# A float32 transformer-like block on one core: the low parts of one weight matrix made by an accumulating DMA instead of a VectorE subtraction

## The chip, the cores and the metric

The kernel runs on one core of a Trainium2 chip. The metric is the device time of one execution in microseconds (us). TensorE (PE) multiplies matrices, VectorE (DVE) and ScalarE (ACT) work element by element, GpSimd (POOL) does small work and can issue DMAs, SyncE (SP) issues nearly all of the DMAs. PEq, ACTq, SPq and POOLq in the profile are the engines' instruction queues.

## The reference, cut to what matters

Two layers (DEPTH = 2) work on 256 tokens of width 1024. Each layer has a feed-forward part, a mixer, a cross attention and a second feed-forward part, each followed by a layer norm. The change lies in the mixer's input product:

```
z = h @ w_in[l]                                   # 256 x 1024 by 1024 x 3072
cb, cc, ch, rq, rf, ri, rg, pu = jnp.split(z, split_at, axis=-1)
y_rec = hgrn2(rq, rf, ri, rg, lbs[l], rec_norm_g[l])   # the recurrence; rq are its queries
```

The 512 columns of w_in that give rq begin at column 768. They are the query weights of the title.

## The kernel before, in words

**Two parts for each float32 factor.** PE multiplies in the format fp32r, which keeps fewer bits than float32. So each factor is split in a rounded part and a rest: `split` (line 60) lets ACT copy the source into the rounded part (line 61, `whi` for weights) and DVE subtract the rounded part from the source (line 62, `wlo`). A product is the sum of three: high by high, high by low, low by high. `product` (line 103) issues all of these matmuls, so that they all stand at line 106.

**Loading weights.** `load` (line 64) brings in a block of 1024 rows by 512 columns as two DMAs of 1 MB on SP (line 76) into `raw`, a ring of 3 buffers. Each raw buffer is split in two halves of 128 x 1024 elements. So a block of 512 columns has four halves, and each half is one ACT copy, one DVE subtraction, one `whi` buffer and one `wlo` buffer, from two rings of 8. Half number n (0 to 3) holds the rows k = 2n and 2n + 1 of the eight groups of 128 rows.

**Products by columns.** In the mixer (line 592) `columns` (line 596) loads a block and then calls `mm_cols` (line 115) for each group of 128 columns. `mm_cols` runs in this order: seven matmuls of `whi` with both parts of the input (k = 0 to 6, 128x512), eight of `wlo` with the input's high part (k = 0 to 7, 128x256), and the last of `whi`. `add` (line 124) then takes the sum out of PSUM: an ACT copy (line 126) and a DVE addition (line 127). The PSUM tiles named `acc` are a ring of 4 buffers.

**Order of the work around the change.** In each layer PE does, one after the other: the end of the first feed-forward part, the keys' first block (`keys`, with `mT`), the four column groups of f (line 628, columns 1280 to 1791; ACT applies a sigmoid at line 617 and DVE makes f and k at lines 619 and 623), the four column groups of q (line 630, columns 768 to 1279, the recurrence's queries), and then the values and the other columns, woven with the recurrence's small matmuls (lines 701 and 736). A scheduler decides the order of each engine's instructions; each engine then runs its own in that order and waits at semaphores. The loads run ahead of the products: while PE multiplies f, the weights of q are split, and the raw weights of the values (columns 1792 on) and of the pool (columns 2816 on) are fetched.

**What POOL does.** It issues 38 small DMAs in the first 50 us, and later runs the power for each layer norm (line 327) and for the recurrence (line 801).

Of the kernel before, what the change touches and what calls it, by code (L numbers as in the profile page):

```python
# [12 lines left out]
ALU = mybir.AluOpType  # L13
# [4 lines left out]
P = 128  # L18
# [5 lines left out]
NK = DM // P  # L24
# [22 lines left out]
def model(ctx: ExitStack, tc: tile.TileContext, t: dict, out: bass.AP):  # L47
    nc = tc.nc
# [11 lines left out]
    def split(hi, lo, src):  # L60
        nc.scalar.copy(hi, src)  # L61
        lows.append(nc.vector.tensor_tensor(lo, src, hi.bitcast(F32), op=ALU.subtract))  # L62

    def load(src, k0, nk, c0, ncol, fine=False, strewn=False):

        hi, lo, todo = [], [], []
        step = 2048 // ncol
        for a in range(k0, k0 + nk, step):  # L70
            raw = wp.tile([P, 2048], F32, tag="raw", name="raw", bufs=3)
            raw = raw.rearrange("p (k c) -> p k c", c=ncol)
            half = step // 2
            part = 1 if fine else step
            for b in range(0, step, part):
                loads.append(nc.sync.dma_start(
                    raw[:, b : b + part, :],
                    src[:, c0 : c0 + ncol].rearrange("(p k) c -> p k c", p=P)[:, a + b : a + b + part, :]
                    if strewn
                    else src[(a + b) * P : (a + b + part) * P, c0 : c0 + ncol].rearrange("(k p) c -> p k c", p=P),  # L80
                ))
            for s in range(2):
                h = wp.tile([P, 1024], F32R, tag="whi", name="whi", bufs=8)
                w = wp.tile([P, 1024], F32R, tag="wlo", name="wlo", bufs=8)
                h = h.rearrange("p (k c) -> p k c", c=ncol)
                w = w.rearrange("p (k c) -> p k c", c=ncol)
                r = raw[:, s * half : (s + 1) * half, :]
                if fine:
                    todo += [(h[:, b, :], w[:, b, :], r[:, b, :]) for b in range(half)]
                else:  # L90
                    split(h, w, r)
                hi.append(h)
                lo.append(w)
        return Weights(hi, lo, half, todo)
# [20 lines left out]
    def mm_cols(w, cols, x):  # L115
        o = acc()
        for k in range(NK - 1):
            product(o, w.at(k, cols)[0], x[:, k], k == 0, False)
        for k in range(NK):
            product(o[:, 0, :], w.at(k, cols)[1], x[:, k, 0, :], False, False)  # L120
        product(o, w.at(NK - 1, cols)[0], x[:, NK - 1], False, True)
        return sums(o)
# [22 lines left out]
    h = [cst.tile([P, DM], F32, name=f"h{i}") for i in range(NT)]  # L145
# [230 lines left out]
    def ffn(l, name, n, pend=None, last=False, early=None):  # L376
        gate, up, down = (t[f"{name}_{x}"][l] for x in ("gate", "up", "down"))
        with tc.tile_pool(name="ffn", bufs=2, reuse_waits="tile") as fp:
# [45 lines left out]
            def first():  # L424

                s = activations()
                wg = load(gate, 0, NK, 0, CHUNK, fine=pend is None)
                wu = load(up, 0, NK, 0, CHUNK) if pend is not None else None

                if pend is None:  # L430
# [8 lines left out]
                    with tc.manual_schedule(engines={E.Activation, E.DVE, E.PE}):  # L439
# [21 lines left out]
                        for k in range(2, NK):  # L461
                            if k + 1 < NK:
                                split(*wg.todo[k + 1])
                            group(k, 0, 1)
                    wu = load(up, 0, NK, 0, CHUNK)
                    ou = all_products(wu)
                    for i in range(NT):
# [124 lines left out]
    def mixer(l, fill):  # L592
        w_in = t["w_in"][l]
        with tc.tile_pool(name="mix", bufs=1, reuse_waits="tile") as mp:

            def columns(c0, ncol, take, behind=lambda p: None, after=None):
                with tc.issue_after(after) if after is not None else nullcontext():
                    w = load(w_in, 0, NK, c0, ncol)
                for j in range(ncol // P):
                    take(j, mm_cols(w, slice(j * P, (j + 1) * P), xT))  # L600
                    if j % 2:
                        behind(j // 2)
                    yield
# [3 lines left out]
            k = mp.tile([P, NT, HEADS, P], F32, name="k")  # L607
# [20 lines left out]
            for _ in columns(1280, 512, lambda j, o: add(f[:, :, j, :], o), ev_f, normed[-1].ins):  # L628
                pass
            for _ in columns(768, 512, lambda j, o: add(q[:, :, j, :], o)):  # L630
                pass
# [36 lines left out]
            def between():  # L668
                yield from values_by_halves()
                yield from columns(2816, 256, lambda j, o: add_forward(pu[:, j, PAD:], o))  # L670
                yield from columns(0, 512, lambda j, o: add_forward(cv[j // 2][:, j % 2, :], o))
                yield from columns(512, 256, lambda j, o: add_forward(u[:, j, 2:], o))
# [51 lines left out]
            for n, c in enumerate(LEVELS):  # L724
                a = 64 // c
# [107 lines left out]
            src = pu  # L833
            for g, w_ in enumerate(WINDOWS):
# [9 lines left out]
                src = d  # L844
# [189 lines left out]
```

## Time and profile before

| what | us |
|---|---|
| median of 3 runs (lowest, highest) | 1090.08 (1089.45, 1090.17) |
| the profiled execution's own time | 1089.82 |
| its span, from first to last instruction | 1088.1 |
| PE busy | 1078.6 |
| DVE busy | 832.7 |
| ACT busy | 573.0 |
| POOL busy | 60.9 |

The span is the time from the first to the last instruction that the profiler recorded; about 1.7 us of the execution lie around it. A row of the timeline has the start in us, the busy time in us, the engine, the line, the operation, output and input tiles and shape, "xN" for N instructions merged into the row, and, in brackets, how long the engine was idle before the row and what ended that. A row of the windows has, for one stretch of the span, its length and then for each engine the busy time in it (with the number of instructions), the granted clock of PE as a share of the full clock, the mean busy share of the 16 DMA engines, and the rate in GB/s. Grouped rows have the number of instructions, the busy time in us and the mean ns of one.

### The profile page before, as it was taken

Reading aid. Unit: us, or ns where it says so; the run is one execution under the profiler, and the core shown is the slowest. Engines: PE = TensorE matmul, PEld = TensorE weight load, DVE = VectorE, ACT = ScalarE, POOL = GpSimd, SP = SyncE. Lnnn points to the kernel's source line nnn. Section 1 sums busy time; section 2 is a strip of 40 time slices with the busy share of each in tenths; the row PEclk is TensorE's granted clock in tenths of the full one; section 3 lists DMA queues with packets and bytes.
Section 4 is the critical chain, followed back from the end, with each engine's and each line's share of the span. In section 5 each row is a group of like instructions: output and inputs, shape, how many; then the busy total and the mean of one; then the engine's idle time right before and its main releaser. Section 6 shows DMA issues by size and latency. Waiting matters only on the chain.

```text
span 1088.1 us, 15589 instructions
## 1 busy us (share of the span) xinstructions
PE 1078.6 (99%) x6051; PEld 954.3 (88%) x6051; DVE 832.7 (77%) x1099; ACT 573.0 (53%) x795; POOL 60.9 (6%) x113
## 2 busy tenths in 40 slices
PE   9999999999999999999999999999999999999997
PEld 7888888989899888888888888898898998888886
DVE  6679677998988877666687655798989888765665
ACT  6456454766557454444455544456764654545450
POOL 9500001000000000000000000010000000000000
PEclk9999999999999999999999999999999999999999
DMA  9986664744475487766488666646536664966641
GB/s 329 300 285 224 220 213 157 247 178 175 173 274 175 164 279 225 236 215 213 155 267 265 222 200 220 227 164 234 185 122 225 235 222 155 286 218 213 221 164 39
DMA packets 122667, 231.85 MB, mean 213 GB/s; under 512 B 6305, under 2 KB 45505, under 8 KB 117473
## 3 DMA queue, kind: packets, MB, share of 16 engines
q1 hardware_dynamic: 120800, 228.48, 63.3%
q0 software_dynamic: 1216, 1.20, 0.4%
q8 instruction: 47, 0.77, 0.3%
q10 hardware_dynamic: 576, 1.18, 0.3%
q14 instruction: 28, 0.22, 0.1%
HBM read 216.15 MB, written 1.05 MB: 200 GB/s over the span
## 4 chain that ended last, share of the span: by engine, by line
PE 99%; DMA 0%; DVE 0%; issue 0%; DVEq 0%
PE acc L106 66%; PE dn L106 30%; PE acc L170 1%; PE dn L736 1%; DMA h<-in_x_dram 0%; PE dn L795 0%; PE dn L794 0%; PE dn L784 0%; PE acc L860 0%; PE dn L701 0%; PE dn L437 0%; DVE h L334 0%; DVE h L330 0%; DVE st L322 0%; DVE h L314 0%
## 5 line engine op out<-in xcount | busy, mean ns | idle before, releaser
L62 DVE TENSOR_TENSOR wlo<-raw,whi 128x1024 fp32r<-128x1024 f32 (+1 forms) x396 | 473.6, 1211 | 179.7 <-ACT whi L61 169.6
L61 ACT CAST whi<-raw 128x1024 fp32r<-128x1024 f32 (+1 forms) x396 | 402.5, 1041 | 334.8 <-PE dn L106 139.5
L106 PE MATMUL acc<-whi,xT 128*128 128x512 f32 x1312 | 395.0, 380 | 0.0
L106 PEld LDWEIGHTS acc<-whi,xT 128*128 128x128 f32 x1312 | 247.8, 189 | 35.2
L106 PE MATMUL acc<-wlo,xT 128*128 128x512 f32 x656 | 248.6, 379 | 0.0
L106 PE MATMUL acc<-xT,whi 128*128 128x512 f32 x576 | 142.1, 382 | 0.0
L106 PEld LDWEIGHTS acc<-wlo,xT 128*128 128x128 f32 x656 | 124.0, 189 | 17.4
L106 PE MATMUL dn<-whi,ah 128*128 128x512 f32 x346 | 131.5, 380 | 0.0
L106 PE MATMUL dn<-wlo,ah 128*128 128x512 f32 x346 | 131.1, 379 | 0.0
L106 PE MATMUL dn<-whi,al 128*128 128x512 f32 x346 | 131.1, 379 | 0.0
L106 PEld LDWEIGHTS acc<-xT,whi 128*128 128x128 f32 x576 | 104.1, 190 | 11.8
L106 PE MATMUL dn<-whi,xT 128*128 128x512 f32 x288 | 88.6, 382 | 0.0
L106 PEld LDWEIGHTS acc<-xT,wlo 128*128 128x128 f32 x576 | 75.5, 191 | 3.9
L106 PE MATMUL acc<-xT,wlo 128*128 128x256 f32 x576 | 75.9, 275 | 0.0
L106 PEld LDWEIGHTS dn<-whi,al 128*128 128x128 f32 x346 | 65.4, 189 | 9.3
L106 PEld LDWEIGHTS dn<-wlo,ah 128*128 128x128 f32 x346 | 65.4, 189 | 9.2
L106 PEld LDWEIGHTS dn<-whi,ah 128*128 128x128 f32 x346 | 65.4, 189 | 9.1
L418 DVE STREAM_TRANSPOSE square<-dealt 128x512 f32<-128x512 f32 x40 | 63.6, 1662 | 0.6 <-DMA dealt<-sg 0.5
L327 POOL TENSOR_TENSOR rs<-rs,nhalf 128x1 f32<-128x1 f32 x16 | 14.9, 929 | 853.7 <-DVE rs L326 853.7
L106 PEld LDWEIGHTS dn<-whi,xT 128*128 128x128 f32 x288 | 54.5, 190 | 7.7 <-DVE xT L62 0.3
L106 PE MATMUL dn<-wlo,xT 128*128 128x512 f32 x144 | 54.6, 379 | 0.0
L320 DVE SCALAR_TENSOR_TENSOR h<-h,dn 128x512 f32<-128x512 f32 x31 | 21.2, 683 | 29.8 <-PE dn L106 29.8
(205 smaller groups left out, 964.5 us busy)
## 6 DMA issues: line engine op xcount, KB each, us to landing
raw<-in_ffn_up_dram SPq DMA_DIRECT2D x44, 1024.0 KB, 5.0
raw<-in_ffn_down_dram SPq DMA_DIRECT2D x44, 1024.0 KB, 5.0
raw<-in_ffn_gate_dram SPq DMA_DIRECT2D x42, 1024.0 KB, 5.0
raw<-in_w_in_dram SPq DMA_DIRECT2D x24, 1024.0 KB, 5.0
dealt<-sg SPq DMA_DIRECT2D x80, 128.0 KB, 3.2
raw<-in_ca_k_dram SPq DMA_DIRECT2D x8, 1024.0 KB, 4.8
raw<-in_w_out_dram SPq DMA_DIRECT2D x8, 1024.0 KB, 4.8
raw<-in_ca_v_dram SPq DMA_DIRECT2D x8, 1024.0 KB, 4.9
```

Source lines behind the costliest of these rows:

```text
L61: nc.scalar.copy(hi, src)
L62: lows.append(nc.vector.tensor_tensor(lo, src, hi.bitcast(F32), op=ALU.subtract))
L106: nc.tensor.matmul(o, w, x, start=start, stop=stop)
L170: nc.tensor.transpose(pt[:, k, :], src[:, (4 * j + k) * P : (4 * j + k + 1) * P], unit)
L320: nc.vector.scalar_tensor_tensor(v, v, ALPHA / scale, sums(y[i][n]), op0=ALU.mult, op1=ALU.add)
L327: nc.gpsimd.tensor_tensor(rs, rs, nhalf[:, 0:1], op=ALU.pow)
L418: nc.vector.transpose(d.rearrange("p k (i b) -> p b k i", b=4), x[:, :, i, :].rearrange("p b (j k) -> p b k j", k=4))
L736: nc.tensor.matmul(o[g, hh, :], kc[:, hh, g], x, start=True, stop=True)
```

## The change

In each layer, for the block of w_in that begins at column 768 and for no other, the low part is no longer made by DVE. ACT writes the rounded part as before, then writes the source times -1, rounded, into the `wlo` buffer, and a DMA issued by POOL reads the same 512 KB of weights once more from HBM and adds them to what stands in `wlo`. The sum is the source less its rounded part, as before.

```diff
-    def load(src, k0, nk, c0, ncol, fine=False, strewn=False):
+    def load(src, k0, nk, c0, ncol, fine=False, strewn=False, summed=False):
...
-                if fine:
+                if summed:
+                    nc.scalar.copy(h, r)
+                    nc.scalar.mul(w, r, -1.0)
+                    nc.gpsimd.dma_start(
+                        w,
+                        src[(a + s * half) * P : (a + (s + 1) * half) * P, c0 : c0 + ncol].rearrange("(k p) c -> p k c", p=P),
+                        accum_op=ALU.add,
+                    )
+                elif fine:
...
-                    w = load(w_in, 0, NK, c0, ncol)
+                    w = load(w_in, 0, NK, c0, ncol, summed=c0 == 768)
```

A block has four halves and there are two layers, so the change concerns 8 halves in all. Built, the changed program has 8 DVE subtractions fewer, 8 ACT instructions more and 8 POOL DMAs more. PE's instructions and their order are the same; the first matmuls on `wlo` in the first column group of q wait for the DMAs where they waited for DVE. On POOL the four DMAs of a layer stand between the power of that layer's first norm (line 327) and the powers of its recurrence (line 801).

## The prediction

> **What bounds the kernel now.** I read the page first, then the windows, then the timelines around the queries' products. The page's busy times, and its chain of work that ended last:
>
> ```profile
> PE 1078.6 (99%) x6051; PEld 954.3 (88%) x6051; DVE 832.7 (77%) x1099; ACT 573.0 (53%) x795; POOL 60.9 (6%) x113
> ...
> PE 99%; DMA 0%; DVE 0%; issue 0%; DVEq 0%
> ```
>
> PE is the bound. The windows show where its idle 9.5 us lie:
>
> ```profile
> 0.00:10.00 10.00, 7.91 (x31) 6.25 (x32) 3.35 (x6) 4.41 (x7) 9.16 (x26) 1.00 0.81 296
> ...
> 192.00:213.00 21.00, 21.00 (x131) 19.29 (x130) 18.55 (x32) 15.13 (x23) 0.00 (x0) 1.00 0.83 278
> 213.00:265.00 52.00, 52.00 (x569) 45.77 (x568) 45.56 (x90) 34.96 (x72) 2.03 (x2) 1.00 0.48 171
> ...
> 950.00:1088.00 138.00, 130.66 (x639) 115.17 (x637) 89.64 (x99) 55.08 (x63) 1.84 (x2) 0.98 0.53 174
> ```
>
> 2.1 us are in the first ten, 7.3 us at the end; in between PE is full. So relief of DVE has next to nothing to win, and a wait that the change puts on PE is paid in full, since no later gap takes it up. The question is only whether the new low parts are there when PE reads them.
>
> **When PE reads them.** PE's timeline, layer 1, then layer 2 (a column group starts with seven `whi` matmuls):
>
> ```profile
> 202.49 1.89 PE L106 MATMUL acc<-xT,whi 128*128 128x512 f32 x8
> 204.22 1.05 PE L106 MATMUL acc<-xT,wlo 128*128 128x256 f32 x8
> 205.11 1.25 PE L106 MATMUL acc<-xT,whi 128*128 128x512 f32 x5
> ```
>
> ```profile
> 740.89 1.05 PE L106 MATMUL acc<-xT,wlo 128*128 128x256 f32 x8
> ```
>
> Eight `wlo` matmuls take 205.11 - 204.22 = 0.89 us, two to a half. Half 0 is read at 204.22, half 2 at 204.67, half 3 at 204.89; in layer 2 half 3 at 741.56.
>
> **Removed and added on DVE and ACT.** The groups between 189 and 206 us, by form:
>
> ```profile
> L62 DVE TENSOR_TENSOR wlo<-raw,whi 128x1024 fp32r<-128x1024 f32 x10 | 11.9, 1219 | 0.4 <-ACT whi L61 0.4
> ...
> L61 ACT CAST whi<-raw 128x1024 fp32r<-128x1024 f32 x8 | 8.0, 1052 | 0.8 <-DMA raw<-in_w_in_dram 0.7
> ...
> L617 ACT ACTIVATE f<-f 128x512 f32<-128x512 f32 x2 | 1.3, 636 | 0.3 <-DVE f L127 0.3
> ...
> L61 ACT CAST kTh<-sums 128x512 fp32r<-128x512 f32 x1 | 0.6, 618 | 0.0
> ```
>
> DVE loses 4 x 1.22 = 4.9 us a layer. On the path that is worth nothing, as PE is full. ACT gains four multiplications. The trace has none of 1024 elements; at 512 an ACTIVATE (636 ns) costs what a cast does (618), so I take the cast's 1.05 us, 4.2 us a layer. ACT is busy 15.13 of 21 us there, so it fits, but it moves the casts and copies behind it. ACT's timeline, and the order of the built program (cast, cast, multiply, copy of sums, multiply, cast of kTh, cast, copy of f, multiply, cast, multiply), give the issue times:
>
> ```profile
> 190.96 2.02 ACT L61 CAST whi<-raw 128x1024 fp32r<-128x1024 f32 x2
> 192.85 0.39 ACT L126 COPY sums<-acc 128x256 f32<-128x256 f32 x1
> 193.96 1.99 ACT L61 CAST whi<-raw 128x1024 fp32r<-128x1024 f32 x2 [0.71 <-DMA raw<-in_w_in_dram]
> ...
> 196.38 0.36 ACT L126 COPY f<-acc 128x256 f32<-128x256 f32 x1
> ```
>
> ```profile
> 729.53 0.40 ACT L126 COPY sums<-acc 128x256 f32<-128x256 f32 x1
> 732.00 1.99 ACT L61 CAST whi<-raw 128x1024 fp32r<-128x1024 f32 x2 [2.07 <-DMA raw<-in_w_in_dram]
> ```
>
> Back to back, each adds about 0.95 us (193.96 + 1.99: two in 1.99). From 192.85 the multiplications end at 193.9, 195.15, 197.85 and 199.75; in layer 2, from 729.53, at 730.6, 731.8, 734.45 and 736.35. The last leaves 5.14 and 5.21 us until PE wants half 3. The copies of f come up to about 3 us later. That costs nothing: the first column's copy ends near 197 while q's first group takes over that `acc` tile at 202.49, and each later group follows 2.6 us on. Were it not so, PE would wait for ACT, at most these 3 us.
>
> **POOL and SP.** POOL's 0 instructions in 192 to 213 (row above) mean that nothing of its own delays the issues; behind them come only the powers of the recurrence, after 213. SP's loads of `raw` that reuse the queries' buffers wait for ACT's multiplication instead of DVE's subtraction: 195.2 and 199.8 instead of the 196.11 and 199.3 below. That shift alone costs nothing, since SP's queue reaches these loads anyway and PE needs the values only at 213. But they are what the new DMAs meet:
>
> ```profile
> 189.11 0.38 SPq L76 DMA_DIRECT2D raw<-in_w_in_dram  x1
> ...
> 193.50 0.38 SPq L76 DMA_DIRECT2D raw<-in_w_in_dram  x1
> ...
> 196.11 3.57 SPq L76 DMA_DIRECT2D raw<-in_w_in_dram  x2
> ```
>
> **The price of an accumulating DMA.** The trace has none. Nearest rows, from the DMA issues, from the queues, and from POOL's loads of `m`:
>
> ```profile
> raw<-in_w_in_dram SPq DMA_DIRECT2D x24, 1024.0 KB, 5.0
> ...
> lng<-in_ln_g_dram SPq DMA_DIRECT2D x8, 512.0 KB, 4.0
> ...
> m<-in_mem_dram POOLq DMA_DIRECT2D x32, 32.0 KB, 6.7
> ```
>
> ```profile
> L186 POOL DMA_DIRECT2D m<-in_mem_dram x32: 582/582/634, 22.2 to 47.4; - x32
> ...
> DMA to landing us min/median/max: 3.6/6.7/8.3
> ```
>
> ```profile
> q1 hardware_dynamic: 120800, 228.48, 63.3%
> q0 software_dynamic: 1216, 1.20, 0.4%
> ```
>
> ```profile
> 189.00:190.00 1.00, 1.00 (x10) 0.97 (x8) 1.00 (x3) 0.27 (x1) 0.00 (x0) 1.00 0.07 29
> 190.00:191.00 1.00, 1.00 (x6) 0.87 (x6) 1.00 (x2) 1.00 (x4) 0.00 (x0) 1.00 0.74 133
> 199.00:200.00 1.00, 1.00 (x10) 1.00 (x9) 0.58 (x2) 0.73 (x2) 0.00 (x0) 1.00 1.07 416
> ```
>
> At a full share the engines move 416 GB/s: 1 MB (1.05e6 bytes) takes 2.5 us, 512 KB 1.26 us. A 1 MB load lands in 5.0: about 1.1 until it moves (the one that SP issues at 189.11), 2.5 moving, 1.4 at the end. POOL's smallest landing, 3.6 us for 32 KB, puts its fixed part near 3.5, so 2.1 before the data and 1.4 behind.
>
> *Low bound:* it moves like a plain copy, 1.26 us each, ahead of all other traffic. The last lands at 199.75 + 3.5 + 1.26 = 204.5, before 204.89: nothing. *Upper bound:* an addition needs both operands, so the DMA must read 512 KB from HBM and 512 KB of `wlo` too, as much as a 1 MB load: 2.5 us each, 10.1 for four. They cannot start before 193.9 + 2.1 = 196.0, and the values' two loads and the pool's (6 us left) share the engines half and half: 196.0 + 16.1 + 1.4 = 213.5, 8.6 us late. *Taken:* the double read, being that of the nearest row of its size in bytes read, and a fifth of the engines for SP's loads meanwhile. The share I chose between none and half: q0's packets held 1.20 MB / 1216 = about 1 KB of 128-byte rows, eight rows to one, while q1's held 1.9 KB, one row. If the queues take turns by packets, POOL's get more than half. Then 196.0 + 10.1 / 0.8 + 1.4 = 210.0, **5.1 us late**.
>
> The Trainium skill, "Collectives: The Full Stack", section "The bandwidth ceiling: the fold count and why AG ≠ RS ≠ AR", says that an add in the DMA path halves the rate because it reads two sources, not because the adding is slow. By it the upper price holds; without it the wait could be nothing. No run here shows it yet.
>
> Layer 2 has the same slack within 0.1 us, and PE and the DMA engines are as full:
>
> ```profile
> 729.00:742.00 13.00, 13.00 (x81) 11.93 (x80) 11.71 (x17) 10.20 (x16) 0.00 (x0) 1.00 0.82 289
> ```
>
> So I take the same wait. **Sum:** 2 x 5.1 = 10.2 on the profiled execution's 1089.8 gives 1100.0; the median of the runs lies 0.3 above that execution, so 1100.3.
>
> **The rivals.**
>
> *A, cheap transfers (27%).* For: the last issue leaves 5.1 us, and a plain 512 KB load lands in 4.0. Against: the engines are 83% busy there already, and POOL's DMAs landed late (6.7) where they were. With plain moves and half the engines, half 3 lands at 207.5: 0 to 2.6 us a layer, 1090.1 to 1095.3. More than half of this (15%) is up to 1.1 us a layer, within 0.2% in all (about the least that a measurement of this kernel tells from no change).
>
> *B, longer waits (18%).* For: the upper bound, 8.6 us a layer, or 1107.3. The new DMAs also hold up the values' raw loads, and ACT's casts of these stand ahead of the copies of q. And PE's clock falls when it idles:
>
> ```profile
> 1080.38 0.28 PE L106 MATMUL acc<-whi,al 128*128 128x256 f32 x1
> ```
>
> ```profile
> 1082.00:1084.00 2.00, 0.00 (x0) 0.00 (x0) 2.00 (x5) 0.00 (x0) 0.92 (x1) 0.79 0.00 0
> 1084.00:1088.00 4.00, 0.00 (x0) 0.00 (x0) 0.84 (x3) 0.00 (x0) 0.00 (x0) 0.50 0.37 133
> ```
>
> PE's last matmul ends at 1080.66; 0.79 means 1.0 until 1083.2, then 0.5: it fell after 2.5 us. In the forecast half 2 comes about 2.2 us late and half 3 keeps PE a further 2.9, so the clock is near its edge. Half speed for as long as it took to fall costs 1.25 a layer. With both, 2 x 9.9 = 19.7: 1109.8. Were the moves twice as slow again, 196.0 + 20.2 / 0.8 + 1.4 = 222.7, 17.8 late: 1125.7.
>
> The Trainium skill, "TensorE: Matmul & The Clock Gate", section "Part 1: The HAM clock gate (the 'warmup' mystery)", halves the clock after an idle window of about 3.4 us and restores it after as much work. By it a drop would cost an estimated 1.7 us a layer; the 2.5 us above fits only if such a window runs free of the matmuls.
>
> *C, faster (3%).* Mechanism: DVE, 4.9 us a layer ahead, ends waits of the recurrence's small matmuls, whose weight loads waited:
>
> ```profile
> PEld dn L736 <- issue: 2.5, 10, 0.3
> ...
> PEld dn L736 <- ACT whi L61: 0.7, 2, 0.3
> PEld dn L736 <- ACT win L843: 0.5, 2, 0.2
> ```
>
> If all 3.7 us went, 1086.4. It decides only if the transfers are wholly hidden, and against it stands that these loads run beside matmuls (PE 52.00 of 52.00).
>
> That the change does not do what it says is not open: the built order has no subtraction for these halves, and PE waits for the DMAs.
>
> **How the numbers follow.** Forecast 52%: 1095 to 1107, likeliest 1100.3. A 27%: 15 within 0.2%, 12 slower. B 18%. C 3%. So faster 0.03, same 0.15, slower 0.82. The range runs from 1090.1, where A begins, to 1112, just past B's 1109.8; C, some of A's hidden end, and B's slower transfers lie outside, less than 2 in 10.
>
> **What would show it.** PE idle ahead of the first `wlo` matmuls of q, near 204.5 and 741, twice 3 to 9 us, ended by DMAs into `wlo`; none there means A. POOL's new issues near 193.9, 195.2, 197.9 and 199.8; if they come later, ACT's walk is wrong. Landings of some 7 to 10 us under the raw loads; 4 to 5 means plain moves. DVE's busy total falls by 9.8 us, ACT's grows by 8.4. A granted clock below 1.00 behind the gaps shows B. Idle time of PE elsewhere would prove wrong that the copies of f are covered.

## The result and the profile after

The change makes the kernel slower: 1114.79 us median of 4 runs (1114.18 to 1115.38) against 1089.76 (1089.40 to 1090.17), a ratio of 1.0229 with a 95% interval of 1.0212 to 1.0247. The prediction was 1100.3 with a range to 1112.0; the time lies above its end. The profiled execution took 1114.18 us with a span of 1112.5, which is 24.4 more than before.

The page of the changed kernel: busy times, two DMA queues (packets, MB, share of the engines), and the chain that ended last.

```profile
PE 1085.7 (98%) x6051; PEld 959.1 (86%) x6051; DVE 824.4 (74%) x1091; ACT 579.2 (52%) x803; POOL 72.6 (7%) x121
...
q1 hardware_dynamic: 120800, 228.48, 62.9%
q0 software_dynamic: 3392, 5.39, 2.5%
...
PE 91%; DVE 3%; DMA 3%; ACT 2%; issue 0%; DVEq 0%; ACTq 0%
```

DVE lost 8.3 us and ACT gained 6.2. Two other numbers tell the story. DMA stands in the chain with 3%, where it had 0%. And PE, whose instructions are the same, is busy 7.1 us longer: the same matmuls ran slower somewhere. The rest of the 24.4 is idle time of PE, which its waits name (us in total, times, longest):

```profile
PE acc L114 <- DMA wlo<-in_w_in_dram: 17.4, 6, 3.5
```

17.4 of waits and 7.1 of longer matmuls are 24.5, against 24.4 of span, so nothing else has to be looked for. The lines of the code have moved by eight: L114 is `product`, L106 before. PE's timeline in layer 1:

```profile
202.25 1.89 PE L114 MATMUL acc<-xT,whi 128*128 128x512 f32 x8
203.98 0.38 PE L114 MATMUL acc<-xT,wlo 128*128 128x256 f32 x2
207.83 0.49 PE L114 MATMUL acc<-xT,wlo 128*128 128x256 f32 x2 [3.46 <-DMA wlo<-in_w_in_dram]
211.34 0.79 PE L114 MATMUL acc<-xT,wlo 128*128 128x256 f32 x2 [3.03 <-DMA wlo<-in_w_in_dram]
214.78 0.79 PE L114 MATMUL acc<-xT,wlo 128*128 128x256 f32 x2 [2.64 <-DMA wlo<-in_w_in_dram]
215.36 3.62 PE L114 MATMUL acc<-xT,whi 128*128 128x512 f32 x8
...
225.37 0.38 PE L114 MATMUL acc<-whi,xT 128*128 128x512 f32 x1
```

Half 0 is there at 203.98; PE then waits for each of the other three halves. Without waits half 3 would have been read 0.67 us after 203.98 (0.89 - 0.22), at 204.65; it is read at 214.78, so it is **10.1 us late**, where 5.1 was forecast. In layer 2 the first `wlo` matmul stands at 753.16, so half 3 would have been read at 753.83; the row below shows it at 763.11, 9.3 late.

```profile
763.11 0.80 PE L114 MATMUL acc<-xT,wlo 128*128 128x256 f32 x2 [2.61 <-DMA wlo<-in_w_in_dram]
```

Then, in layer 1, eight `whi` matmuls take 3.62 us that took 1.89 at 202.25: the clock. The windows, with the granted clock and the DMA engines' share and rate as the last three columns:

```profile
196.00:198.00 2.00, 2.00 (x15) 1.87 (x14) 0.56 (x2) 2.00 (x4) 0.58 (x2) 1.00 1.06 365
198.00:204.00 6.00, 6.00 (x38) 5.46 (x37) 2.70 (x6) 5.97 (x9) 2.26 (x2) 1.00 1.06 235
...
206.00:209.00 3.00, 0.49 (x2) 0.30 (x2) 0.00 (x0) 0.13 (x1) 0.00 (x0) 1.00 1.11 242
209.00:212.00 3.00, 0.66 (x2) 0.50 (x2) 1.52 (x3) 2.38 (x3) 0.00 (x0) 0.51 1.10 232
...
215.00:219.00 4.00, 4.00 (x12) 3.27 (x13) 2.16 (x3) 0.94 (x2) 0.00 (x0) 0.50 0.59 229
219.00:220.00 1.00, 1.00 (x9) 1.00 (x9) 0.00 (x0) 0.00 (x0) 0.00 (x0) 0.86 0.61 86
220.00:226.00 6.00, 6.00 (x37) 5.49 (x36) 3.48 (x9) 3.32 (x5) 0.00 (x0) 1.00 0.42 160
```

The clock falls at about 209.0, 4.6 us after PE's steady work ended at 204.37 (207.83 less the 3.46 of idle time), with only two matmuls in between, and comes back at about 219.3 (0.86 means that 0.28 of that microsecond was still at 0.5). In layer 2 the windows put the fall at 758.6, 5.1 us after the steady work ended, and the return at 768.8, 5.7 us after 763.11. From 214.78 to 219.3 PE works 4.5 us at half speed, which costs 2.25; the values' first product then begins 12.4 us later than before, counted from the first `wlo` matmul (225.37 - 203.98 = 21.4 against 213.19 - 204.22 = 9.0 before), which is 10.1 + 2.3. Before, PE's timeline had the values' first product here:

```profile
213.19 0.38 PE L106 MATMUL acc<-whi,xT 128*128 128x512 f32 x1
```

In layer 2 the same sum is 9.3 + 2.9 = 12.2. Together 24.6: the 19.4 of lateness are the 17.4 of idle time and 2.0 by which the `wlo` matmuls between the waits took longer. Most of these 2.0 are not the clock's: a pair that stands alone takes 0.38 to 0.49 us at the full clock, where two in a row of eight take 0.22.

The DMA columns are worth as much attention. The engines are fully busy from 196 on, at 365 GB/s first and at 232 to 242 in the rows from 198 to 212: busy, but moving two thirds as much. POOL's issues and the landing (KB each, median us):

```profile
194.00 2.48 POOL L91 DMA_DIRECT2D wlo<-in_w_in_dram  x2 [9.70 <-ACT sums L134]
197.89 1.17 POOL L91 DMA_DIRECT2D wlo<-in_w_in_dram  x1 [1.42 <-ACT wlo L90]
199.78 1.19 POOL L91 DMA_DIRECT2D wlo<-in_w_in_dram  x1 [0.71 <-ACT f L134]
```

```profile
wlo<-in_w_in_dram POOLq DMA_DIRECT2D x8, 512.0 KB, 12.6
```

### The profile page after: what moved, and what is told of

It reads as the page before. It is cut to its first block, busy times and chain, and to the rows that moved or that the text cites. A ratio compares the mean times of both kernels' runs of the same rounds, so it can differ in the third digit from the quotient of the medians.

```text
span 1112.5 us, 15603 instructions
## 1 busy us (share of the span) xinstructions
PE 1085.7 (98%) x6051; PEld 959.1 (86%) x6051; DVE 824.4 (74%) x1091; ACT 579.2 (52%) x803; POOL 72.6 (7%) x121
## 3 DMA queue, kind: packets, MB, share of 16 engines
q0 software_dynamic: 3392, 5.39, 2.5%
## 4 chain that ended last, share of the span: by engine, by line
PE 91%; DVE 3%; DMA 3%; ACT 2%; issue 0%; DVEq 0%; ACTq 0%
PE acc L114 61%; PE dn L114 28%; DMA wlo<-in_w_in_dram 3%; PE acc L178 1%; DVE wlo L62 1%; ACT wlo L90 1%; ACT whi L89 1%; DVE h L342 1%; PE dn L744 1%; DVE h L328 0%; DVE h L338 0%; PE dn L803 0%; DMA h<-in_x_dram 0%; DVE st L330 0%; DVE xT L62 0%
## 5 line engine op out<-in xcount | busy, mean ns | idle before, releaser
L62 DVE TENSOR_TENSOR wlo<-raw,whi 128x1024 fp32r<-128x1024 f32 (+1 forms) x388 | 463.7, 1211 | 178.9 <-ACT whi L61 170.2
L61 ACT CAST whi<-raw 128x1024 fp32r<-128x1024 f32 (+1 forms) x388 | 394.2, 1041 | 340.8 <-PE dn L114 153.9
L114 PE MATMUL acc<-whi,xT 128*128 128x512 f32 x1312 | 395.0, 380 | 0.0
L114 PEld LDWEIGHTS acc<-whi,xT 128*128 128x128 f32 x1312 | 247.8, 189 | 35.2
L114 PE MATMUL acc<-wlo,xT 128*128 128x512 f32 x656 | 248.6, 379 | 0.0
L114 PE MATMUL acc<-xT,whi 128*128 128x512 f32 x576 | 145.6, 389 | 0.0
L114 PEld LDWEIGHTS acc<-wlo,xT 128*128 128x128 f32 x656 | 124.0, 189 | 17.5
L114 PE MATMUL dn<-whi,ah 128*128 128x512 f32 x346 | 131.5, 380 | 0.0
L114 PE MATMUL dn<-wlo,ah 128*128 128x512 f32 x346 | 131.1, 379 | 0.0
L114 PE MATMUL dn<-whi,al 128*128 128x512 f32 x346 | 131.1, 379 | 0.0
L114 PEld LDWEIGHTS acc<-xT,whi 128*128 128x128 f32 x576 | 106.5, 194 | 12.6
L114 PEld LDWEIGHTS acc<-xT,wlo 128*128 128x128 f32 x576 | 78.0, 196 | 22.9 <-DMA wlo<-in_w_in_dram 18.8
L114 PE MATMUL acc<-xT,wlo 128*128 128x256 f32 x576 | 79.8, 281 | 17.4 <-DMA wlo<-in_w_in_dram 17.4
L114 PE MATMUL dn<-whi,xT 128*128 128x512 f32 x288 | 88.5, 381 | 0.0
L114 PEld LDWEIGHTS dn<-whi,al 128*128 128x128 f32 x346 | 65.4, 189 | 9.3
L114 PEld LDWEIGHTS dn<-wlo,ah 128*128 128x128 f32 x346 | 65.4, 189 | 9.2
L114 PEld LDWEIGHTS dn<-whi,ah 128*128 128x128 f32 x346 | 65.4, 189 | 9.1
L114 PEld LDWEIGHTS dn<-whi,xT 128*128 128x128 f32 x288 | 54.5, 190 | 7.7 <-DVE xT L62 0.2
L114 PE MATMUL dn<-wlo,xT 128*128 128x512 f32 x144 | 54.6, 379 | 0.0
```

Source lines behind the costliest of these rows:

```text
L114: nc.tensor.matmul(o, w, x, start=start, stop=stop)
```

## The experiments

Times are medians. Each ratio is to the kernel before on the same chip, with its 95% interval. All are edits of the changed kernel except the third. A line of dots in a code cut stands for lines left out.

**1. DVE adds what the DMA added.** ACT's work stays, in nearly the same order; the addition goes back to DVE.

```diff
-                    nc.gpsimd.dma_start(
-                        w,
...
-                        accum_op=ALU.add,
-                    )
+                    lows.append(nc.vector.tensor_tensor(w, r, w.bitcast(F32), op=ALU.add))
```

> ACT still writes the negated rounded part, but DVE adds the weights to it in place of the DMA: 4 additions a layer on DVE at 1.22 us, no POOL DMA. Theory D (the DMAs are the whole cost): 1089 to 1091 us, no wait of PE before the queries' low parts. Rival A (ACT's four multiplications of 1.08 us and the copies that they push back cost something themselves): 1092 us or more, with PE waits ended by ACT.

Measured: 1090.17 us, ratio 1.0006 (0.9996 to 1.0015). The eight multiplications on ACT and the moved copies cost nothing that can be told from noise. The whole loss belongs to the DMAs.

**2. The DMA copies and doesn't add.** The low parts are then the weights themselves, so the rest term of the product is left out; transfers, issues and waits stay.

```diff
-                        accum_op=ALU.add,
```

> The same POOL DMAs at the same places, but as plain copies: the low parts are then the weights themselves, so the added term is left out. Theory D (an accumulating DMA reads two operands, so it fills the engines for 2.5 us where a copy does for 1.26): the last of four lands 5 us earlier than in the changed kernel, near 207 to 210 in place of 214.7, PE waits 2 to 5 us a layer in place of 10.1 and 9.3, the clock stays up in most of it, and the time is 1094 to 1101 us. Rival P (POOL's path is slow for any DMA of this size): landings of 9 to 15 us as before, 1112 to 1116 us.

Measured: 1100.25 us, ratio 1.0101 (1.0085 to 1.0117). The waits of PE and the DMA issues of this kernel:

```profile
PE acc L113 <- DMA wlo<-in_w_in_dram: 6.5, 4, 2.2
```

```profile
wlo<-in_w_in_dram POOLq DMA_DIRECT2D x8, 512.0 KB, 7.9
```

The adding is worth 14.5 of the 25 us. The other 10.5 are lost with plain copies too, which move 2 MB more per layer through engines that were 83% busy in that stretch.

**3. The price alone.** The kernel before, with six transfers of the same 512 KB behind its last work, each waiting for the one ahead: by SP, by POOL, by POOL adding, and the last three into the format of `wlo` (copy, add, add).

```diff
+    with tc.issue_after(outs[-1].ins):
+        nc.sync.dma_start(one, part)
+    nc.gpsimd.dma_start(one, part)
+    nc.gpsimd.dma_start(one, part, accum_op=ALU.add)
+    nc.scalar.mul(two, one, -1.0)
+    nc.gpsimd.dma_start(two, part)
+    nc.gpsimd.dma_start(two, part, accum_op=ALU.add)
+    nc.gpsimd.dma_start(two, part, accum_op=ALU.add)
```

> The kernel before, and behind its end, one after the other with nothing else on the engines: 512 KB of the same weights by SP as a copy; by POOL as a copy and as an accumulation into a float32 tile; then by POOL as a copy and as two accumulations into an fp32r tile. Theory D: SP's copy lands in 3.6 us, POOL's in 4.5 to 5.5, an accumulation 1.3 us later than POOL's copy (6 to 7). Rival P: POOL's copy takes as long as the accumulation. Rival F (the conversion to fp32r is the slow part): the fp32r ones land later than the float32 ones by 1 us or more. The run is longer than before by 25 to 40 us at its end, which says nothing.

Measured: 1122.94 us in one execution, with the added transfers all behind the kernel's own work. From issue to landing: copy by SP 3.8 us, copy by POOL 4.1, addition by POOL 6.1; into `wlo`'s format 4.1, 6.1 and 6.0. So neither POOL's path (0.3) nor the conversion (0.0) is what is dear, but the addition, by 2.0 us. POOL's copy came faster than expected (4.5 to 5.5) and the addition cost more on top of it than expected (1.3). POOL's issues (columns as in the timeline, L1014 and L1017 add, L1013 and L1016 copy), and a window in the second addition:

```profile
1089.58 0.78 POOL L1013 DMA_DIRECT2D one<-in_w_in_dram  x1 [6.76 <-DMA one<-in_w_in_dram]
1093.98 1.24 POOL L1014 DMA_DIRECT2D one<-in_w_in_dram  x1 [3.62 <-DMA one<-in_w_in_dram]
1101.82 0.74 POOL L1016 DMA_DIRECT2D two<-in_w_in_dram  x1 [6.60 <-ACT two L1015]
1106.23 1.20 POOL L1017 DMA_DIRECT2D two<-in_w_in_dram  x1 [3.67 <-DMA two<-in_w_in_dram]
```

```profile
1110.00:1111.00 1.00, 0.00 (x0) 0.00 (x0) 0.00 (x0) 0.00 (x0) 0.00 (x0) 0.50 1.11 205
```

An addition takes 1.2 us to issue, a copy 0.75. At a full share the engines add at 205 GB/s, half of the 416 that the loads reach in the kernel before: 512 KB take 2.6 us.

**4. SP's loads held back.** The values' second load waits until the last addition has landed, by a transfer of one column that reads the last `wlo`; all that stands behind it in SP's queue waits too (in layer 1 SP issues nothing between 193.2 and 210.0).

```diff
+            if c0 == 1792 and a:
+                held = nc.sync.dma_start(rows[:, 0:1], added[-1][1][:, 0, 0:1].bitcast(F32))
...
+              with tc.issue_after(held.ins) if c0 == 1792 and a else nullcontext():
```

> The changed kernel, with SP's queue held before the values' second raw load until the layer's last accumulating DMA has landed (a DMA of 4 bytes a partition that reads its output stands in front). So only the values' first load still runs beside the four. Theory C (the four DMAs are slow because SP's loads take turns with them): each needs 2.5 to 2.6 us of the engines at the 203 GB/s that one reached alone, the last lands near 209, PE waits 4 to 5 us a layer in place of 10.1 and 9.3, and the time is 1098 to 1102 us. Rival Q (POOL's DMAs follow each other at 3.5 us each whatever else runs): the last still lands near 214, and the time is 1111 us or more, the held loads adding to it.

Measured: 1106.78 us, ratio 1.0159 (1.0142 to 1.0176), above what was expected. PE's timeline in layer 1, a window, and PE's waits:

```profile
203.92 0.38 PE L117 MATMUL acc<-xT,wlo 128*128 128x256 f32 x2
204.64 0.49 PE L117 MATMUL acc<-xT,wlo 128*128 128x256 f32 x2 [0.34 <-DMA wlo<-in_w_in_dram]
207.35 0.79 PE L117 MATMUL acc<-xT,wlo 128*128 128x256 f32 x2 [2.22 <-DMA wlo<-in_w_in_dram]
209.89 0.79 PE L117 MATMUL acc<-xT,wlo 128*128 128x256 f32 x2 [1.75 <-DMA wlo<-in_w_in_dram]
```

```profile
205.00:208.00 3.00, 0.78 (x4) 0.50 (x2) 1.76 (x4) 0.21 (x1) 0.00 (x0) 0.89 1.14 206
```

```profile
PE acc L117 <- DMA wlo<-in_w_in_dram: 8.7, 6, 2.2
...
PE dn L712 <- DVE q L138: 1.2, 1, 1.2
```

With the engines to themselves the additions land 2.7 and 2.5 us apart instead of 3.5 and 3.4, and half 3 comes 5.3 us late instead of 10.1. So SP's loads took about half of the lateness. The time fell by only 8.0 us, though, as PE was still busy 5.1 us longer than before (the clock fell in both layers), and the loads that were held came late for others: ACT's casts of them wait 3.77 us for raw data, the copies of q stand behind these casts, and PE has a wait for q that wasn't there.

**5. The wait filled with matmuls.** Forty matmuls that nobody uses stand ahead of the first `wlo` matmuls in each layer, so that PE doesn't idle.

```diff
+        spare = acc((P, 512), "dn") if idle else None
+        for n in range(idle):
+            product(spare, w.at(n % 7, cols)[0], x[:, n % 7].rearrange("p h c -> p (h c)"), True, True)
```

> The changed kernel with 40 matmuls of 128x512 that nothing reads, put between the queries' first seven high matmuls and the first low one; 8.6 us at full clock, less than the wait of 10.1 and 9.3 us. Theory K (the queries' matmuls ran at half speed because PE idled): the clock stays at 1.00, the two losses of 2.3 and 2.9 us go, and the time is 1109 to 1111 us. Rival S (they ran slowly because the DMA traffic slows PE's reads): the matmuls behind the wait are still slow and the time is 1114 to 1116 us.

Measured: 1110.35 us, ratio 1.0190 (1.0175 to 1.0206): with 80 matmuls more it is 4.4 us faster than the changed kernel. PE's timeline and a window:

```profile
204.33 8.80 PE L114 MATMUL dn<-xT,whi 128*128 128x512 f32 x40
212.96 0.83 PE L114 MATMUL acc<-xT,wlo 128*128 128x256 f32 x6
215.46 0.49 PE L114 MATMUL acc<-xT,wlo 128*128 128x256 f32 x2 [1.67 <-DMA wlo<-in_w_in_dram]
215.79 1.89 PE L114 MATMUL acc<-xT,whi 128*128 128x512 f32 x8
```

```profile
206.00:214.00 8.00, 7.79 (x40) 6.71 (x38) 3.39 (x7) 3.31 (x4) 0.00 (x0) 1.00 1.10 243
```

The DMAs run as in the changed kernel (1.10, 243 GB/s) and half 3 lands as late (215.46), but the clock stays at 1.00 and the `whi` matmuls behind it take 1.89. So it was PE's idling that made it slow, not the transfers beside it, and the clock is some 5 us of the 25.

**6. Two halves instead of four.** Only the halves of the first raw load are made by DMA.

```diff
-                if summed:
+                if summed and a == k0:
```

> Only the first raw load of the block (halves 0 and 1) uses multiplication and DMA, the second is subtracted by DVE. Theory C: two DMAs land where the first two of four did or earlier, near 203 and 206 to 207.8; half 1 is read at 204.4, so PE waits 2 to 3.4 us a layer, the clock hardly falls, and the time is 1094 to 1098 us. Rival L (the cost is proportional to the number of DMAs): half of 25 us, 1102 us.

Measured: 1099.60 us, ratio 1.0090 (1.0075 to 1.0105), 1.6 above what was expected. PE waits once a layer, for half 1:

```profile
PE acc L114 <- DMA wlo<-in_w_in_dram: 6.1, 2, 3.1
```

The span is 8.5 longer than before: these 6.1, and 2.3 of longer matmuls, most of it in layer 2, where this wait was enough for the clock to fall, as PE's timeline shows:

```profile
747.84 0.94 PE L114 MATMUL acc<-xT,wlo 128*128 128x256 f32 x6 [3.02 <-DMA wlo<-in_w_in_dram]
748.62 3.22 PE L114 MATMUL acc<-xT,whi 128*128 128x512 f32 x8
```

Eight `whi` matmuls take 3.22 us instead of 1.89. In layer 1 a wait of 3.1 did not do that: the granted clock is 1.00 from 203 to 215. The other three executions of this kernel took 1.2 to 2.5 us longer, at a mean granted clock of 0.995 or 0.996 against 0.997 in this one, so whether such a wait costs the clock may differ from one execution to the next. The expectation had put hardly anything on the clock.

**7. The low parts asked for later.** All 28 `whi` matmuls of q's four column groups come first, then the 32 of `wlo`, then the last four of `whi`.

```diff
+            for j in range(4):
+                for kk in range(NK - 1):
+                    product(os[j], w.at(kk, cs[j])[0], xT[:, kk], kk == 0, False)
+            for n in range(4):
+                for j in range(4):
+                    for kk in (2 * n, 2 * n + 1):
+                        product(os[j][:, 0, :], w.at(kk, cs[j])[1], xT[:, kk, 0, :], False, False)
...
```

> The changed kernel with another order of the queries' matmuls: the 28 high ones of all four column groups first, then the low ones half by half, then the last high ones. The work is the same. The DMAs land as before (203, 207.8, 211.3, 214.7). The 28 high matmuls last until about 208.8, half 3 is wanted at 211.5, so PE waits about 3 us a layer in pieces too short for the clock to fall: 1095 to 1098 us under theories C and K together. If the lost time lay in something other than PE's wait for the low parts, the time would stay at 1110 us or more.

Measured: 1110.48 us, ratio 1.0192 (1.0177 to 1.0207). That missed by 12 us. PE's waits, and ACT's timeline:

```profile
PE acc L114 <- DVE q L135: 6.8, 2, 3.5
PE acc L114 <- DMA wlo<-in_w_in_dram: 5.9, 3, 3.0
```

```profile
215.92 1.99 ACT L61 CAST whi<-raw 128x1024 fp32r<-128x1024 f32 x2 [3.32 <-DMA raw<-in_w_in_dram]
218.49 1.04 ACT L61 CAST whi<-raw 128x1024 fp32r<-128x1024 f32 x1 [0.58 <-DMA raw<-in_w_in_dram]
219.44 1.19 ACT L134 COPY q<-acc 128x256 f32<-128x256 f32 x4
```

The wait for the low parts fell from 17.4 to 5.9, but a new one of 6.8 came. The four copies of q are now all due at the same time, and in ACT's order they stand behind casts of the next weights, which themselves wait for raw data that the additions have delayed.

**8. Both 4 and 7.**

> The held load and the order with the high matmuls first together. Theory C: the last DMA lands near 209 while half 3 is wanted at 211.5, so PE does not wait for the low parts: 1090 to 1092 us, if the held loads still come in time for the values at 213. Rival Q: 1096 us or more. Nothing here can pass the kernel before, whose PE is full.

Measured: 1113.97 us, ratio 1.0222 (1.0206 to 1.0237); a miss by over 20 us. No wait for the low parts is left, but the same casts now wait for loads that are held, and q's copies behind them. PE's waits:

```profile
PE acc L117 <- DVE q L138: 19.9, 2, 10.4
```

**9 and 10. The casts behind q's copies.** As 7 and as 8, with the casts of the values' second load and of the pool's load put behind q's last copy on ACT.

```diff
+                elif c0 in (1792, 2816) and (a or c0 == 2816):
+                    with tc.issue_after(copies[-1].ins):
+                        nc.scalar.copy(h, r)
...
```

> The kernel of e7_highs_first, with the casts of the values' second load and of the pooling's load issued on ACT behind the last of q's four copies; nothing else is moved. Theory O (the wait of 3.5 us for q in e7 is ACT's order: q's copies stood behind casts that waited for their raw data): the wait for q falls to under 0.6 us a layer, the waits for the low parts stay as they were (0.6 + 2.3 us a layer), the clock falls for less than in e7, and the time comes to 1095 to 1098 us. Rival X (the four accumulators taken at once are what holds the values' first product, whatever stands on ACT): the wait for q stays at 2 us or more a layer, 1104 to 1110.

> As e9, with SP's queue also held before the values' second load until the last accumulating DMA has landed, as in e8. Theory O: no wait for the low parts, none for q of over 0.6 us; what is left is a wait of PE for the values' held second load, 1 to 2 us a layer: 1091 to 1096 us. Rival X: PE waits for q as long as in e8 (10 us a layer), 1108 to 1114.

Measured: 1104.23 us, ratio 1.0129 (1.0114 to 1.0144), and 1099.46, ratio 1.0087 (1.0070 to 1.0104). PE's waits in the ninth:

```profile
PE acc L118 <- DMA wlo<-in_w_in_dram: 6.3, 3, 3.2
PE dn L806 <- DVE q L773: 1.7, 2, 0.9
```

and in the tenth:

```profile
PE dn L761 <- DVE q L730: 3.2, 2, 1.7
PE dn L809 <- DVE q L776: 2.0, 2, 1.3
PE acc L121 <- DVE wlo L104: 1.6, 2, 0.8
...
PE acc L121 <- ACT whi L103: 1.2, 2, 1.0
PE acc L121 <- DVE q L142: 0.5, 2, 0.3
```

The wait of 6.8 and 19.9 for q's tiles is gone or 0.5, so it was ACT's order, as theory O had it. Both times are above what was expected all the same. In the ninth the clock still fell in both layers, for 7.0 us of longer matmuls. In the tenth the low parts cost PE nothing and the clock hardly moved, and yet 9.6 us are lost: the values' halves are late (the waits for `whi` and `wlo`), and the queries that DVE works on behind their subtractions (the waits for q).

One table over all of them but the third, worked out from the first lines of each page. *Idle* is the span less PE's busy time, *longer* PE's busy time, both less those of the kernel before (9.5 and 1078.6; in the fifth also less 80 matmuls at 8.80 / 40 = 0.22 us). Not all of *longer* is the clock: each wait that cuts a row of `wlo` matmuls in two adds some 0.2 to 0.3 us.

| kernel | span | idle | longer |
|---|---|---|---|
| changed | 1112.5 | 17.3 | 7.1 |
| 1, DVE adds | 1089.3 | 1.0 | 0.2 |
| 2, copies | 1097.3 | 6.4 | 2.8 |
| 4, held | 1103.8 | 10.6 | 5.1 |
| 5, filled | 1109.4 | 3.3 | 0.4 |
| 6, two halves | 1096.6 | 6.2 | 2.3 |
| 7, highs first | 1108.5 | 12.7 | 7.7 |
| 8, both | 1112.8 | 19.9 | 4.8 |
| 9 | 1103.2 | 8.1 | 7.0 |
| 10 | 1097.9 | 8.7 | 1.1 |

No version with these DMAs comes near the kernel before. None could have beaten it by much, since PE was full there.

## Why the prediction was wrong

**What held.** PE is the bound and pays a wait in full: 17.4 of waits and 7.1 of longer matmuls make the 24.4, and in the windows PE is full elsewhere, but for the first and last microseconds as before. The walk of ACT gave issues at 193.9, 195.2, 197.9 and 199.8; they came at 194.0 (two, 1.24 each), 197.89 and 199.78. That ACT's and DVE's part costs nothing is shown by the first experiment. Layer 2 goes as layer 1, within 0.9 us. DVE's total was to fall by 9.8 and ACT's to grow by 8.4; the 8.3 and 6.2 have the sign, and what took up the rest wasn't traced. The price of one addition, "the double read, 2.5 us", was 2.6, and with the 3.5 of POOL's fixed part it would land in 6.0 alone; 6.1 and 6.0 were measured. That these agree so well is in part luck: POOL's copy landed in 4.1, and less 1.26 that leaves 2.8 for the fixed part of a copy, not 3.5. The Trainium skill, "Collectives: The Full Stack", section "The bandwidth ceiling: the fold count and why AG ≠ RS ≠ AR", has an add in the DMA path halve the rate of a collective; 205 GB/s against 416 is the same half for the transfer of this kernel.

**What failed.** Three steps. Two make the lateness of half 3, for which the forecast had 196.0 + 10.1 / 0.8 + 1.4 = 210.0: the start and SP's share, 198.1 + 10.4 / 0.68 + 1.4 = 214.8 by the figures below. The third is the cost of the clock, which the forecast put at nothing.

| term, layer 1 | forecast | measured |
|---|---|---|
| the additions start | 196.0 | about 198.1 |
| four prices | 10.1 | 10.4 |
| SP's share meanwhile | 20% | up to 32% |
| half 3 lands | 210.0 | 214.7 |
| half 3 late, both layers | 10.2 | 19.4 |
| clock behind the waits, both layers | 0 | 5.2 |

*The start.* "193.9 + 2.1 = 196.0" took the fixed part of a transfer on idle engines. The rate stays at 365 GB/s until 198, which is a raw load's, so the additions had to let that load move first. The fourth experiment gives the same start: half 3 landed at 209.9 there, and less 1.4 and 10.4 that is 198.1; its first addition landed 8.1 us after its issue, 2.0 later than alone. These 2.1 us are of the size of one raw load's move; that it alone makes them was read from the rows and not tried.

*SP's share.* "A fifth of the engines" rested on packets of eight rows in POOL's queue. The new packets hold (5.39 - 1.20) MB / (3392 - 1216) = 1.9 KB, one row, like SP's. From 198.1 to 214.7 - 1.4 = 213.3 the four additions would have needed 10.4 of 15.2 us alone, which leaves a third for SP's loads. That is what queues would give that take turns packet by packet, if one packet costs twice the other. The turns are inferred; that the additions take 3.4 to 3.5 us each beside SP's loads and 2.5 to 2.7 without them is measured. Counted in bytes the share is smaller: 239 GB/s from 198 to 213.3 are 3.66 MB, less the additions' 2.10 MB that is 1.56 MB for SP, or 3.7 us at 416 GB/s, a quarter of the time. What the rest was spent on stays open. The row for q0 described its small rows of 128 bytes, and I carried it over to transfers with rows of another size.

The upper bound of 213.5 was no bound either, because it had the early start in it.

*The clock.* The sum has no term for it, although the forecast saw the clock "near its edge". With the lateness twice as long it fell in both layers. Rival B had the mechanism and put 1.25 us a layer on it, half of the 2.5 that the clock took to fall at the kernel's end. What counts is how long PE must work until it is back, 4.5 and 5.7 us in the changed kernel, and half of that is 2.3 and 2.9. The Trainium skill, "TensorE: Matmul & The Clock Gate", section "Part 1: The HAM clock gate (the 'warmup' mystery)", gives about 3.4 us for both ways. Here the fall came 2.5 us after PE's last work at the end of the kernel before and 4.6 and 5.1 us after the steady work in the changed kernel, and the return after 4.5 and 5.7 us of work, so for this kernel the measured times decide. The 3.4 us do come back in the second and the sixth experiment, where the clock fell only after PE was at work again: it was low from 209.4 to 212.8 and from 749.0 to 752.4, which cost 1.7 us each.

Rival A's cheap moves fell by the third experiment. Rival C needed wholly hidden transfers; in the tenth, where no `wlo` was late, other loads were.

## What to carry to other kernels

Before work is moved from a vector engine to a DMA, add up what the DMA engines must then move in that stretch: here 10.4 us a layer went into 21 us that were already 83% busy, just ahead of a deadline of 5 us, and where their lateness was hidden (the tenth experiment) the raw loads that they delayed still cost 9.6 us. A wait on a full PE can also cost the clock: here a single wait of 3.0 us was enough in one layer and one of 3.1 in the other was not, and a fall cost half of the time that PE then worked at half speed, 1.7 to 2.9 us. And when a wait is moved away, look at what is queued behind the next one that it meets: two of the attempts to hide these DMAs were lost to casts that stood ahead of four short copies.

## What was not expected of the hardware

- An addition by DMA takes POOL 1.2 us to issue, a copy 0.75, and POOL's loads of 32 KB in the kernel before took 0.58.
- The conversion to PE's format in the DMA costs nothing (4.1 against 4.1 us, 6.1 and 6.0 against 6.1).
- A busy share of 1.06 to 1.14 says nothing on the rate: 365 to 416 GB/s with loads alone, 205 and 206 with additions alone, 232 to 243 with both.
